# One substitution on 64 partitions for the last two delta rule heads, and the order of adds, casts and splits at the ends of the MLPs and of the last head

## The chip, the cores and the metric

One Trainium2 chip, one core. The metric is device time in microseconds (us). TensorE (PE) multiplies matrices, PEld is its weight load, VectorE (DVE) and ScalarE (ACT) work on tiles, GpSimd (POOL) and SyncE (SP) here mostly issue DMAs. Each engine runs its own instructions in the order in which they were laid down, and waits where an operand or a buffer isn't there yet.

## The reference

Two transformer blocks on 512 tokens of width 1024, in fp32. Cut to what the change touches:

```python
# block 1
h = rmsnorm(x, norm_mix)
gu, gv, q, k, v, gate, b_logit, a_logit = split_cols(h @ w_in, IN_SIZES)
y_a = chunk_spatial_gating(gu, gv, ...)
o = gated_delta_rule(q, k, v, g, beta)     # 4 heads of 128, chunks of 64 tokens
y_b = rmsnorm(o, dn_onorm) * silu(gate)
x = x + concat([y_a, y_b]) @ w_out
m = rmsnorm(mem, norm_mem)                 # 256 memory rows
x = x + cross_attention(rmsnorm(x, norm_xa), m @ w_k, m @ w_v)
x = x + square(relu(rmsnorm(x, norm_ffn) @ w1)) @ w2
# block 2
x = x + mixer2(rmsnorm(x, norm_mix_g))     # mLSTM and sliding window attention
x = x + square(relu(rmsnorm(x, norm_mlp_g) @ w_up)) @ w_down
x = x + sigmoid(rmsnorm(x, norm_ple_g) @ w_ple_gate) * (p @ w_ple_proj)
return rmsnorm(x, final_norm_g)
# in gated_delta_rule, per head and chunk c:
m = strict_lower((k*beta) @ k.T * decay);  a = m + eye(64)
sol = triangular_solve(a, rhs)             # rhs = [v*beta, k*beta*exp(decay)]
```

The kernel takes chunks of 128 tokens, which gives the same o, and inverts their `a`: the 16x16 blocks on the diagonal by forward substitution, then blocks of 32, 64 and 128 by matmuls. A head has four chunks and so 32 blocks of 16x16.

## The kernel before

Every fp32 product is three matmuls on a high and a low half of both operands (`mm3`, L282 to L284). A weight comes by DMA on SP into a raw tile `wr` (L260), ACT casts it to `wh` (L263), DVE subtracts to get `wl` (L264). A granule is 1024x256 of a weight in two such pieces of 128x1024 (512 KB), or one piece for `w_out_b` and `w_out_a`. Outside the MLPs there are two `wr` buffers and three each of `wh` and `wl` (`wtiles`), so a load starts when the `wl` of two pieces before it is done. With each granule the kernel also issues `rate` jobs that build sums of the MLP weights in DRAM by DMA (`job`, `sum_jobs`).

The program is written step by step, and a list scheduler lays the instructions down on each engine, by its own estimates and priorities. `behind(f)` issues what f does after the last matmul so far, `hold(n)` keeps matmuls until n products later, `issue_after(i)` holds an instruction behind another one. With `high_priority(n)` instructions are placed as if they stood n places earlier in the program.

Delta rule (`deltanet`, `dn_head`): a head first makes its scaled q, k, v, the matrix M and QKT (L601 to L646). Then the 16x16 blocks are multiplied out of M on PE (L661), copied by ACT (L671), and spread by four DMAs of 8 KB (L678) so that one block lies on each of 32 partitions. There 15 pairs of DVE operations (L681 multiply, L683 subtract) invert all 32 blocks at once. Four DMAs (L685) bring the result back, L687 places it into `dTb` (T_), and L661, L711, L715 and L720 build up the inverse. Four steps over chunks follow (L735 to L754), the norm and the gate (L758 to L768) and the transposes in `fin` (L773) with the split into `yb` (L327, L328).

Around heads 2 and 3 the matmuls of the memory fill PE: four granules of `xa_wk`, each giving two tiles of 128x256, and four of `xa_wv` (`memory`). The keys are scaled by `bc`, made by `tok_bc`: DVE copies (L354), PE transposes twice (L357), ACT copies (L359), then DVE scales each key tile out of its PSUM bank (L812). Three PSUM banks (`psd`) go round. In the kernel before head 2's substitution and chain stand beside the keys, head 3's beside the values. Then `w_out_b` follows, whose last quarter of the sum (k = 3) needs head 3.

The second GEMM of an MLP (`st_gemm`) makes seven products per granule, added into `x_fm` by DVE (L982) from three PSUM tiles. At the end of an MLP `post` splits each finished tile for the next norm (L327, L328) and sums squares (`sq_acc`, L337 on ACT, L338 on DVE). At the end of MLP 1 this feeds `between`, at the end of MLP 2 `tail`, whose `ple` splits the input p (L324, L325).

Of the kernel before, what the change touches and what calls it, by code (L numbers as in the profile page):

```python
# [12 lines left out]
AF = mybir.ActivationFunctionType  # L13
ALU = mybir.AluOpType
# [18 lines left out]
C_ONORM = C_CONV2 + 32  # L33
# [32 lines left out]
class Kern:  # L66
# [199 lines left out]

    def wgran(self, name, g, n=256, nk=8, pieces=None):

        if self.wx is None:
            self.job()  # L270
        src = self.D[name]
        parts = []
        for h in range(nk // 4):
            parts.append(self.wload(src[g, h], 4, n, pieces if h == 0 else None))
# [45 lines left out]
    def split_sb(self, hi, lo, src, scale=None):  # L320

        nc = self.nc
        if scale is None:
            nc.scalar.copy(hi, src)  # L324
            nc.vector.tensor_tensor(out=lo, in0=src, in1=hi.bitcast(F32), op=ALU.subtract)  # L325
        else:
            nc.scalar.activation(hi, src, AF.Copy, scale=scale)  # L327
            nc.vector.scalar_tensor_tensor(out=lo, in0=src, scalar=scale, in1=hi.bitcast(F32), op0=ALU.mult, op1=ALU.subtract)  # L328

    def sq_acc(self, acc, src, k, scale=None, n=T):  # L330
# [141 lines left out]
    def deltanet(self, xh, xl, rs, bc, mix, mem):  # L472
        nc, mp = self.nc, self.mp
# [16 lines left out]
        qk, v, fins = {}, {}, []  # L490
# [17 lines left out]

        def do_prep(h):
            return self.dn_head(h, *qk[h], v[h], pr, gate, yb_h, yb_l)  # L510

        def do_head(h):
            steps = do_prep(h)
            next(steps)
            fins.append(next(steps))

# [5 lines left out]
        pr = self.dn_prep(ba)  # L522
# [62 lines left out]

    def dn_head(self, h, q, k, v, pr, gate, yb_h, yb_l):

# [84 lines left out]
        Vt, Mo = b4("dV"), b4("dA" + e, 1)  # L672
        bl = lambda t, o: t[0:32].rearrange("p b c -> p (b c)")[:, o:o + 256].rearrange("p (r c) -> p r c", r=16)
        Lb, Tb, Ob = bl(Vt, 0), bl(Vt, 256), bl(Mo, 0)
        V.memset(Tb, 0.0)
        V.memset(flat(Tb)[:, 0::17], 1.0)
        for b in range(NB):
            nc.sync.dma_start(Lb[8 * b:8 * b + 8], Lp[:, b])  # L678
        for j in range(15):
            n, m = 15 - j, j + 1  # L680
            nc.vector.tensor_tensor(out=Ob[:, :n, :m], in0=Lb[:, m:, j:m].broadcast_to([32, n, m]),  # L681
               in1=Tb[:, j:m, :m].broadcast_to([32, n, m]), op=ALU.mult)
            nc.vector.tensor_tensor(out=Tb[:, m:, :m], in0=Tb[:, m:, :m], in1=Ob[:, :n, :m], op=ALU.subtract)  # L683
# [95 lines left out]
    def w_out1(self):  # L779

        xh, xl = self.pair((9, 10)), self.pair((11, 12))
        acc = self.new_acc()

        def ev(o, ps):
            self.add_res(o, ps)
            self.norm_tile(o, xh, xl, acc, "norm_xa")

        for g in range(4):
            self.proj_fm(self.wgran("w_out_b", g, nk=4), *self.yb, (2 * g, 2 * g + 1), ev)
        self.dump("x1", self.x)  # L790
        return xh, xl, acc
# [135 lines left out]
    def st_weights(self, name, g):  # L927
# [36 lines left out]
    def st_gemm(self, name, g, H, o1, post):  # L964
# [60 lines left out]
    def between(self):  # L1025
# [7 lines left out]
        def ev(o):  # L1033
            nonlocal ops
            if o == 0:
                ops = self.pair((2, 3)), self.pair((5, 6)), self.new_acc(), self.t(self.fp, [P, T], "acc2", bufs=1)
            xh, xl, acc, acc2 = ops
            self.split_sb(xh[o], xl[o], self.x[:, o], g12[:, o:o + 1])
            self.sq_acc(acc, self.x[:, o], o)
            self.sq_acc(acc2, self.x[:, o], o, scale=self.vcol("norm_final", o))  # L1040

        def fin():
            self.dump("x3", self.x)
            xh, xl, acc, acc2 = ops
            r1 = self.tok_rs(acc, "rs", power=True)
            ps = self.pss()
            for b in range(NB):
                nc.tensor.matmul(ps[:, b:b + 1], acc2[:, b * P:(b + 1) * P], self.ones[:, 0:1], start=True, stop=True)
            v = self.t(self.tp, [P, NB], "rs2v")
# [331 lines left out]
    def tail(self):  # L1381
# [5 lines left out]
        def ev(o):  # L1387
            nonlocal ops
            if o == 0:
                ops = self.pair((0, 1)), self.pair((4, 7)), self.new_acc()  # L1390
            self.norm_tile(o, *ops, "norm_ple_g_2")

        def ple():
# [207 lines left out]
```

## Time and profile before

| | |
|---|---|
| median of 3 runs | 1700.75 us (1698.43 to 1703.73) |
| profiled execution | 1699.93 us, span 1698.1 us |
| granted TensorE clock | 1.000 over the span |
| PE busy | 1677.7 us, 99% |
| DVE busy | 1207.7 us, 71% |
| ACT busy | 821.5 us, 48% |
| DMA | 205.63 MB, mean 121 GB/s |

A busy share counts overlapping matmuls as one stretch. PE is the engine that is nearly always busy, so the places where it stands still are read one by one: the number in square brackets in a row of the timeline is how long the engine was idle before the instruction, and what ended that.

### The profile page before, as it was taken

How to read it: one execution, taken by the hardware profiler on the slowest of the kernel's cores; microseconds unless marked ns; L12 is line 12 of the kernel's file. 1: busy time of each engine (PE TensorE's matmuls, PEld its weight loads, DVE VectorE, ACT ScalarE, POOL GpSimd, SP SyncE). 2: the span in 40 equal slices, each digit the busy share in tenths (PEclk: the TensorE clock that was granted, in tenths of full speed). 3: DMA queues.
4: the chain of work that ended last, by engine and by line, in shares of the span. 5: the costliest groups of instructions: out<-in, count | busy, mean ns of one | idle time of the engine just before them, and what ended most of it. 6: DMA issues, size and time to landing. Idle time of an engine off the chain costs nothing.

```text
span 1698.1 us, 25916 instructions
## 1 busy us (share of the span) xinstructions
PE 1677.7 (99%) x9916; PEld 1455.5 (86%) x9916; DVE 1207.7 (71%) x2521; ACT 821.5 (48%) x1462; POOL 72.2 (4%) x92
## 2 busy tenths in 40 slices
PE   9999999999999999999999999999999999999998
PEld 8988898887898989889988887788888989898987
DVE  6988886656686868688845569865566767676865
ACT  5355755444444444454444457654234444444554
POOL 0200001000000000000000000000000000000000
PEclk9999999999999999999999999999999999999999
DMA  6321366545546464423333332334464464644331
GB/s 203 101 76 52 96 154 180 135 99 174 121 130 170 127 170 128 132 92 110 103 90 97 100 88 69 94 88 115 118 189 126 130 172 124 172 125 133 100 112 50
DMA packets 81947, 205.63 MB, mean 121 GB/s; under 512 B 13088, under 2 KB 14240, under 8 KB 81824
## 3 DMA queue, kind: packets, MB, share of 16 engines
q1 hardware_dynamic: 62672, 169.29, 31.9%
q0 software_dynamic: 9216, 16.78, 7.1%
q10 hardware_dynamic: 9936, 17.91, 3.8%
q8 instruction: 78, 1.28, 0.3%
q14 instruction: 45, 0.37, 0.1%
HBM read 201.59 MB, written 35.65 MB: 140 GB/s over the span
## 4 chain that ended last, share of the span: by engine, by line
PE 88%; DVE 7%; ACT 2%; issue 1%; DMA 1%; SPq 0%; ACTq 0%; DVEq 0%
PE psd L283 21%; PE psd L284 21%; PE psd L282 21%; PE x L282 5%; PE x L283 5%; PE x L284 5%; DVE wl L264 1%; PE c L661 1%; PE c L607 1%; PE lg L1344 1%; PE po L1371 1%; ACT wh L263 1%; DVE S L437 1%; PE m L1265 1%; DVE acc L338 1%
## 5 line engine op out<-in xcount | busy, mean ns | idle before, releaser
L284 PE MATMUL psd<-S,wl 128*128 128x512 f32 (+1 forms) x1256 | 484.1, 386 | 2.6 <-DVE wl L264 2.5
L282 PE MATMUL psd<-S,wh 128*128 128x512 f32 (+1 forms) x1256 | 483.1, 385 | 0.7 <-ACT S L327 0.7
L283 PE MATMUL psd<-S,wh 128*128 128x512 f32 (+1 forms) x1192 | 458.6, 385 | 1.1 <-DVE S L328 0.8
L284 PEld LDWEIGHTS psd<-S,wl 128*128 128x128 f32 x1256 | 236.3, 188 | 48.1 <-DVE wl L264 3.7
L282 PEld LDWEIGHTS psd<-S,wh 128*128 128x128 f32 x1256 | 236.5, 188 | 45.6 <-ACT S L327 1.1
L264 DVE TENSOR_TENSOR wl<-wr,wh 128x1024 fp32r<-128x1024 f32 (+2 forms) x160 | 192.2, 1201 | 116.3 <-ACT wh L263 115.6
L283 PEld LDWEIGHTS psd<-S,wh 128*128 128x128 f32 x1192 | 224.2, 188 | 44.3 <-DVE S L325 1.5
L263 ACT CAST wh<-wr 128x1024 fp32r<-128x1024 f32 (+2 forms) x160 | 163.9, 1026 | 154.7 <-PE psd L283 107.2
L284 PE MATMUL psd<-wh,S 128*128 128x256 f32 (+2 forms) x480 | 135.8, 283 | 0.0
L282 PE MATMUL psd<-wh,S 128*128 128x256 f32 (+2 forms) x480 | 135.7, 283 | 0.0
L283 PE MATMUL psd<-wl,S 128*128 128x256 f32 (+2 forms) x480 | 135.2, 282 | 0.0
L282 PE MATMUL x<-S,wh 128*128 128x256 f32 x452 | 128.0, 285 | 2.9 <-DVE x_fm L982 2.8
L283 PE MATMUL x<-S,wh 128*128 128x256 f32 x452 | 126.5, 281 | 0.0
L284 PE MATMUL x<-S,wl 128*128 128x256 f32 x452 | 126.0, 280 | 0.0
L283 PE MATMUL psd<-S,whx 128*128 128x512 f32 (+1 forms) x296 | 107.8, 364 | 1.0 <-DVE S L325 0.9
L282 PE MATMUL psd<-S,whx 128*128 128x512 f32 (+1 forms) x296 | 107.8, 365 | 0.0
L284 PE MATMUL psd<-S,wlx 128*128 128x512 f32 (+1 forms) x296 | 107.5, 363 | 0.0
L982 DVE TENSOR_TENSOR x_fm<-x_fm,x 128x256 f32<-128x256 f32 x192 | 78.5, 415 | 27.4 <-PE x L284 27.1
L282 PEld LDWEIGHTS psd<-wh,S 128*128 128x128 f32 x480 | 90.4, 189 | 0.3
L283 PEld LDWEIGHTS psd<-wl,S 128*128 128x128 f32 x480 | 90.3, 188 | 0.3
L284 PEld LDWEIGHTS psd<-wh,S 128*128 128x128 f32 x480 | 90.4, 188 | 0.1
L282 PEld LDWEIGHTS x<-S,wh 128*128 128x128 f32 x452 | 84.8, 188 | 5.8 <-DVE x_fm L982 3.1
(455 smaller groups left out, 3176.3 us busy)
## 6 DMA issues: line engine op xcount, KB each, us to landing
wrx<-in_ffn_w_dram SPq DMA_DIRECT2D x32, 512.0 KB
wrx<-in_w_up_dram SPq DMA_DIRECT2D x20, 512.0 KB
wr<-in_w_in_qk_dram SPq DMA_DIRECT2D x16, 512.0 KB
sums_ffn_w<-in_ffn_w_dram ACTq DMA_DIRECT2D x32, 256.0 KB
wr<-in_ffn_w_dram SPq DMA_DIRECT2D x16, 512.0 KB
sums_w_down<-in_w_down_dram ACTq DMA_DIRECT2D x32, 256.0 KB
wr<-in_w_in_v_dram SPq DMA_DIRECT2D x12, 512.0 KB
wr<-in_w_up_dram SPq DMA_DIRECT2D x12, 512.0 KB
```

Source lines behind the costliest of these rows:

```text
L263: self.last_cast = nc.scalar.copy(hi[:, c], raw[:, c])
L264: nc.vector.tensor_tensor(out=lo[:, c], in0=raw[:, c], in1=hi[:, c].bitcast(F32), op=ALU.subtract)
L282: mm(ps, ah, bh, start=first, stop=False, skip_group_check=more)
L283: mm(ps, ah, bl, start=False, stop=False, skip_group_check=more)
L284: self.last_mm = mm(ps, al, bh, start=False, stop=last, skip_group_check=more)
L338: nc.vector.tensor_tensor(out=acc, in0=acc, in1=sq, op=ALU.add)
L437: nc.vector.tensor_scalar(out=d, in0=d, scalar1=ag[:, j, 0:1], scalar2=r[:, j:j + 1], op0=ALU.subtract, op1=ALU.mult)
L607: nc.tensor.matmul(blk(ps, b), lhs(b), rhs(b), start=True, stop=True)
L661: nc.tensor.matmul(ps[:, b * n:(b + 1) * n], lhs[:, b], rhs(b), start=True, stop=True)
L982: TT(out=x[n][t], in0=x[n][t], in1=ps, op=op)
L1265: nc.tensor.matmul(pX[:, :W], PT[:, tt], va[:, tt], start=True, stop=True)
L1344: nc.tensor.matmul(ps[:, i, K0:], qs[:, 2 * e2 + i, cs], kd[:, w, kc], start=(w == 0), stop=(w == 1))
```

## The change

Heads 2 and 3 put their blocks into one tile: head 2's on partitions 0 to 31, head 3's on 32 to 63. The 15 pairs run once, on 64 partitions, after both heads' blocks have arrived. Head 2's chain now runs beside head 3's. `do_head` is still used for heads 0 and 1. The first granule of `w_out_b` does k = 0, 1, 2 for both of its tiles and then k = 3 for both, and the cast of its second granule is held behind the cast of `yb`. In the MLPs the adds into `x_fm` and the weight splits get priority 400, the norm splits at the end 200, and p's splits and the copies of the p product 400. The matmuls of the statistics in `between` are held for 8 products, `tok_bc` for 21 instead of 16. Line numbers of the changed kernel differ from those before: L264 is L265 there, L338 L340, L354 L356, L357 L359, L661 L670, L681 and L683 are L696 and L698, L685 and L687 are L701 and L704, L812 is L840, L982 is L1013.

```diff
-    def wload(self, src, kt, n, pieces=None):
+    def wload(self, src, kt, n, pieces=None, behind=None):
...
-            self.last_cast = nc.scalar.copy(hi[:, c], raw[:, c])
+            with self.tc.issue_after(behind.ins) if behind else nullcontext():
+                self.last_cast = nc.scalar.copy(hi[:, c], raw[:, c])
...
-    def norm_tile(self, k, xh, xl, acc, gname):
-
-        self.split_sb(xh[k], xl[k], self.x[:, k], self.vcol(gname, k))
+    def norm_tile(self, k, xh, xl, acc, gname, ahead=0):
+
+        with self.tc.high_priority(ahead):
+            self.split_sb(xh[k], xl[k], self.x[:, k], self.vcol(gname, k))
...
-        do_head(2)
+
+        two = do_prep(2, 64)
+        next(two)
         do_wa(1)
-        prep = do_prep(3)
-        next(prep)
+        both = next(two)
+        three = do_prep(3, 64, both)
+        for steps in (three, three, two, three):
+            next(steps)
         do_wa(2)
         do_wa(3)
...
-        fins.append(next(prep))
-        for _ in range(5):
+        for steps in (two, three):
+            fins.append(next(steps))
+            next(mem)
+        for _ in range(3):
             next(mem)
...
+        tiles = first or (Vt, Mo)
+        Lb, Tb, Ob = bl(tiles[0], 0), bl(tiles[0], 256), bl(tiles[1], 0)
+        at = 32 if first else 0
...
         for b in range(NB):
-            nc.sync.dma_start(Lb[8 * b:8 * b + 8], Lp[:, b])
...
+            nc.sync.dma_start(Lb[at + 8 * b:at + 8 * b + 8], Lp[:, b])
+        if rows == 64 and not first:
+            yield tiles
+        else:
+            for j in range(15):
+                n, m = 15 - j, j + 1
+                nc.vector.tensor_tensor(out=Ob[:, :n, :m], in0=Lb[:, m:, j:m].broadcast_to([rows, n, m]),
+                   in1=Tb[:, j:m, :m].broadcast_to([rows, n, m]), op=ALU.mult)
+                nc.vector.tensor_tensor(out=Tb[:, m:, :m], in0=Tb[:, m:, :m], in1=Ob[:, :n, :m], op=ALU.subtract)
+            yield
         for b in range(NB):
-            nc.sync.dma_start(Rp[:, b], Tb[8 * b:8 * b + 8])
+            nc.sync.dma_start(Rp[:, b], Tb[at + 8 * b:at + 8 * b + 8])
+        yield
...
+        wh, wl = self.wgran("w_out_b", 0, nk=4)
+        (yh, yl), ps = self.yb, [self.psd() for _ in range(2)]
+        for ks in ((0, 1, 2), (3,)):
+            for j in range(2):
+                for k in ks:
+                    c = slice(j * P, (j + 1) * P)
+                    self.mm3(ps[j], wh[k][:, c], wl[k][:, c], yh[k], yl[k], k == 0, k == 3)
...
+            w = self.wgran("w_out_b", g, nk=4, behind=self.yb_cast if g == 1 else None)
...
         def split(raw, hi, lo, c=slice(0, 2)):
-            self.split_sb(hi[:, c], lo[:, c], raw[:, c])
+            with self.tc.high_priority(400):
+                self.split_sb(hi[:, c], lo[:, c], raw[:, c])
...
         def add(n, t, ps, op=ALU.add):
-            TT(out=x[n][t], in0=x[n][t], in1=ps, op=op)
+            with self.tc.high_priority(400):
+                TT(out=x[n][t], in0=x[n][t], in1=ps, op=op)
...
-            with self.hold(16):
+            with self.hold(21):
```

On DVE, where the second piece of the first key granule is turned into `wl` (`wl_2756` before, `wl_2630` after), before:

```order
L681 TENSOR_TENSOR dA_402_2284<-dV_2283 32x3x13
L643 TENSOR_TENSOR dM_2576<-c_462_2571,slg_2546 128x512
L683 TENSOR_TENSOR dV_2283<-dV_2283,dA_402_2284 32x3x13
L646 TENSOR_TENSOR QKT_2583<-c_464_2578,slg_2546 128x512
L681 TENSOR_TENSOR dA_402_2284<-dV_2283 32x2x14
L189 TENSOR_TENSOR rsmt_2726<-rsmy_2725 128x2
L264 TENSOR_TENSOR wl_2756<-wr_2754,wh_2755 128x1024
```

After:

```order
L386 SCALAR_TENSOR_TENSOR dq_2093<-sq_2139,e_371_2134 128x512
L473 TENSOR_TENSOR x_fm<-psd_2488,x_fm 128x512
L771 TENSOR_TENSOR do_1817<-do_1817,c_317_1855 128x128
L265 TENSOR_TENSOR wl_2630<-wr_2628,wh_2629 128x1024
L778 TENSOR_TENSOR dso_1860<-dso_1860,dsc_1866 128x4
L783 TENSOR_TENSOR do_1817<-do_1817,gate_713 128x512
```

The piece stood behind 13 pairs of head 2's substitution and M and QKT of head 3; now it stands ahead of both, among the end of head 1.

On PE, where the key scale is transposed (`pss`); `psd_3036` before and `psd_2858` after is the first tile of the second key granule. Before:

```order
L284 MATMUL psd_3036<-S_477_2662,wl_3026 128x256
L282 MATMUL psd_3036<-S_477_2662,wh_3025 128x256
L357 MATMUL pss_2740<-masks,e_500_2738 128x128 x2
L283 MATMUL psd_3036<-S_478_2663,wh_3025 128x256
L284 MATMUL psd_3036<-S_477_2662,wl_3026 128x256
```

After:

```order
L284 MATMUL psd_2858<-S_444_2537,wh_2853 128x256
L285 MATMUL psd_2858<-S_443_2536,wl_2854 128x256
L359 MATMUL pss_2614<-masks,e_466_2612 128x128 x2
L283 MATMUL psd_2887<-S_443_2536,wh_2847 128x256
L284 MATMUL psd_2887<-S_444_2537,wh_2847 128x256
```

The transposes moved from the middle of the third key tile to its end; the next matmul writes a fourth tile, into the bank that the first one holds until it is scaled.

On DVE, the same place and the start of the scaled tiles, after (before, the copy `e` had only the `wl` of the piece that PE was using ahead of it):

```order
L189 TENSOR_TENSOR rsmt_2600<-rsmy_2599 128x2
L265 TENSOR_TENSOR wl_3066<-wr_3064,wh_3065 128x1024
L190 SCALAR_TENSOR_TENSOR rsmt_2600<-rsmt_2600,rsmv_2596 128x2
L329 SCALAR_TENSOR_TENSOR S_177_1232<-c_481_2692,vec,S_176_1231 128x512
L191 SCALAR_TENSOR_TENSOR rsmy_2599<-rsmt_2600,rsmy_2599 128x2
L356 COPY e_466_2612<-rsmy_2599 128x256
L840 TENSOR_TENSOR e_478_2659<-psd_2634,bc_2617 128x256
L696 TENSOR_TENSOR dA_407_2318<-dV_2317 64x15
```

The copy stands behind `wl_3066`, the first piece of the third key granule, and the shared substitution begins behind the first scaled tile. It ends on DVE here (`wl_3217` is the second piece of the first value granule):

```order
L265 TENSOR_TENSOR wl_3211<-wr_3209,wh_3210 128x1024
L698 TENSOR_TENSOR dV_2317<-dV_2317,dA_407_2318 64x5x11
L326 TENSOR_TENSOR S_470_2620<-e_581_3130,S_469_2619 128x256
...
L696 TENSOR_TENSOR dA_407_2318<-dV_2317 64x15
L698 TENSOR_TENSOR dV_2317<-dV_2317,dA_407_2318 64x15
L674 TENSOR_TENSOR dA_407_2318<-dM_2255,masks 128x512
L265 TENSOR_TENSOR wl_3217<-wr_3215,wh_3216 128x1024
```

On DVE at the end of MLP 1 (`x_7767` before is `x_7735` after), before:

```order
L328 SCALAR_TENSOR_TENSOR S_1202_7591<-x_fm,g_804_4657,S_1200_7589 128x512
L325 TENSOR_TENSOR wl_7764<-wr_7742,wh_7763 128x1024
L338 TENSOR_TENSOR acc_7593<-acc_7593,sq_7736 128x512
L338 TENSOR_TENSOR acc_1205_7594<-acc_1205_7594,sq_7739 128x512
L982 TENSOR_TENSOR x_fm<-x_fm,x_7767 128x256
L982 TENSOR_TENSOR x_fm<-x_fm,x_7768 128x256
```

After:

```order
L329 SCALAR_TENSOR_TENSOR S_1202_7559<-x_fm,g_804_4625,S_1200_7557 128x512
L1013 TENSOR_TENSOR x_fm<-x_fm,x_7600 128x256
L326 TENSOR_TENSOR wlx_7848<-wrx_7846,whx_7847 128x1024
L326 TENSOR_TENSOR wl_7732<-wr_7710,wh_7731 128x1024
L1013 TENSOR_TENSOR x_fm<-x_fm,x_7735 128x256
```

The sums of squares of that tile moved to some 25 places later, and the add stands behind weight splits alone.

## Rows read from the trace of the kernel before

**Rows 1.** The page's list of engines: busy time, share of the span, instructions.

```profile
PE 1677.7 (99%) x9916; PEld 1455.5 (86%) x9916; DVE 1207.7 (71%) x2521; ACT 821.5 (48%) x1462; POOL 72.2 (4%) x92
```

**Rows 2.** The waits of PE over the whole span: engine, what it was to do, what ended the wait; us in total, times, longest.

```profile
PE x L282 <- DVE x_fm L982: 2.8, 3, 1.7
PE psd L284 <- DVE wl L264: 2.5, 3, 1.2
```

**Rows 3.** A table by stretch: the stretch and its length, busy time of PE, PEld, DVE, ACT and POOL (instructions), granted clock, DMA share, GB/s. The stretches are the key granules, the value granules, the first of `w_out_b` and the end of MLP 1.

```profile
212.47:252.02 39.55, 37.50 (x316) 35.92 (x314) 33.84 (x125) 19.71 (x49) 3.24 (x4) 1.00 0.62 155
252.02:287.94 35.92, 35.57 (x297) 33.80 (x296) 22.91 (x64) 19.88 (x45) 3.23 (x4) 1.00 0.65 169
287.94:320.00 32.06, 30.53 (x132) 24.23 (x131) 23.77 (x32) 17.27 (x25) 4.06 (x5) 1.00 0.78 191
740.00:775.00 35.00, 33.06 (x272) 32.28 (x271) 32.40 (x55) 20.29 (x29) 0.00 (x0) 1.00 0.31 98
```

**Rows 4.** The timeline of all engines in the first key granule.

```profile
217.40 0.36 PE L283 MATMUL psd<-S,wh 128*128 128x256 f32 x1
217.66 1.21 DVE L264 TENSOR_TENSOR wl<-wr,wh 128x1024 fp32r<-128x1024 f32 x1
218.93 0.33 SPq L260 DMA_DIRECT2D wr<-in_xa_wk_dram  x1
218.93 0.39 PE L284 MATMUL psd<-S,wl 128*128 128x256 f32 x1 [1.16 <-DVE wl L264]
```

**Rows 5.** The timeline of ACT over the same granule and the next: the casts of the two pieces concerned, and the copy of the key scale.

```profile
203.79 1.06 ACT L263 CAST wh<-wr 128x1024 fp32r<-128x1024 f32 x1 [0.34 <-PE psd L283]
222.93 1.05 ACT L263 CAST wh<-wr 128x1024 fp32r<-128x1024 f32 x1
224.25 0.38 ACT L359 COPY bc<-pss 128x256 f32<-128x256 f32 x1 [0.27 <-PE pss L357]
```

**Rows 6.** The timeline of all engines in the second key granule, around the transposes of the key scale.

```profile
223.43 0.29 DVE L354 COPY e<-rsmy 128x256 f32<-128x256 f32 x1
223.77 0.44 PE L357 MATMUL pss<-masks,e 128*128 128x128 f32 x2
224.28 0.28 PE L282 MATMUL psd<-S,wh 128*128 128x256 f32 x1
224.29 1.22 DVE L264 TENSOR_TENSOR wl<-wr,wh 128x1024 fp32r<-128x1024 f32 x1
224.40 0.28 PE L283 MATMUL psd<-S,wh 128*128 128x256 f32 x1
225.56 0.39 PE L284 MATMUL psd<-S,wl 128*128 128x256 f32 x1 [0.89 <-DVE wl L264]
225.63 0.42 DVE L812 TENSOR_TENSOR e<-psd,bc 128x256 f32<-128x256 f32 x1
```

**Rows 7.** The substitutions of heads 2 and 3, from the view of line L681: count, shortest, median and longest duration in ns, first and last start.

```profile
L681 DVE TENSOR_TENSOR dA<-dV x30: 155/192/214, 204.6 to 249.6; 32x15 f32<-32x15 f32 x4, 32x28 f32<-32x28 f32 x4, 32x39 f32<-32x39 f32 x4, 32x48 f32<-32x48 f32 x4
```

**Rows 8.** The timeline of DVE: head 3's last subtract, and the placing of its T_.

```profile
249.76 0.16 DVE L683 TENSOR_TENSOR dV<-dV,dA 32x15 f32<-32x15 f32 x1
254.96 0.28 DVE L687 TENSOR_TENSOR dTb<-dY,masks 128x128 f32<-128x128 f32 x1
```

**Rows 9.** The timeline of SP's queue: start, time to the end of the last of the group, count. L260 loads pieces of weights, L685 brings T_ back.

```profile
241.27 6.56 SPq L260 DMA_DIRECT2D wr<-in_xa_wv_dram  x3
249.99 2.68 SPq L685 DMA_DIRECT2D dY<-dV  x4
...
282.54 0.33 SPq L260 DMA_DIRECT2D wr<-in_w_out_b_dram  x1
```

**Rows 10.** The timeline of ACT: casts that waited for their load, and the cast of head 3's `yb` (L327).

```profile
245.17 1.05 ACT L263 CAST wh<-wr 128x1024 fp32r<-128x1024 f32 x1 [0.78 <-DMA wr<-in_xa_wv_dram]
252.66 1.05 ACT L263 CAST wh<-wr 128x1024 fp32r<-128x1024 f32 x1 [0.77 <-DMA wr<-in_xa_wv_dram]
289.20 1.05 ACT L263 CAST wh<-wr 128x1024 fp32r<-128x1024 f32 x1 [2.07 <-DMA wr<-in_w_out_b_dram]
290.15 0.68 ACT L327 ACTIVATE S<-c,vec 128x512 fp32r<-128x512 f32 x1
```

**Rows 11.** The timeline of PE and DVE in the first granule of `w_out_b`.

```profile
290.28 1.23 DVE L264 TENSOR_TENSOR wl<-wr,wh 128x1024 fp32r<-128x1024 f32 x1 [4.53 <-ACT wh L263]
290.88 0.50 PE L282 MATMUL psd<-S,wh 128*128 128x512 f32 x1 [0.70 <-ACT S L327]
291.42 0.74 DVE L328 SCALAR_TENSOR_TENSOR S<-c,vec,S 128x512 fp32r<-128x512 f32 x1
292.22 0.50 PE L283 MATMUL psd<-S,wh 128*128 128x512 f32 x1 [0.83 <-DVE S L328]
```

**Rows 12.** The timeline of PE and DVE at the end of MLP 1.

```profile
757.24 1.28 DVE L338 TENSOR_TENSOR acc<-acc,sq 128x512 f32<-128x512 f32 x2
758.45 0.74 DVE L982 TENSOR_TENSOR x_fm<-x_fm,x 128x256 f32<-128x256 f32 x2
758.91 0.38 PE L282 MATMUL x<-S,wh 128*128 128x256 f32 x1 [1.69 <-DVE x_fm L982]
```

**Rows 13.** The timeline of PE at the end of MLP 2 and in the first product of `ple`.

```profile
1623.41 0.36 PE L282 MATMUL x<-S,wh 128*128 128x256 f32 x1 [0.86 <-DVE x_fm L982]
...
1631.83 0.50 PE L283 MATMUL psd<-S,whx 128*128 128x512 f32 x1 [0.95 <-DVE S L325]
```

More of the change, by code (lines that the diff above doesn't have):

```diff
@@ L273, in wgran @@
         for h in range(nk // 4):
-            parts.append(self.wload(src[g, h], 4, n, pieces if h == 0 else None))
+            parts.append(self.wload(src[g, h], 4, n, pieces if h == 0 else None, behind))
         hi = [parts[k // 4][0][:, k % 4] for k in range(nk)]
@@ L323, in split_sb @@
         if scale is None:
-            nc.scalar.copy(hi, src)
+            cast = nc.scalar.copy(hi, src)
             nc.vector.tensor_tensor(out=lo, in0=src, in1=hi.bitcast(F32), op=ALU.subtract)
         else:
-            nc.scalar.activation(hi, src, AF.Copy, scale=scale)
+            cast = nc.scalar.activation(hi, src, AF.Copy, scale=scale)
             nc.vector.scalar_tensor_tensor(out=lo, in0=src, scalar=scale, in1=hi.bitcast(F32), op0=ALU.mult, op1=ALU.subtract)
+        return cast
     def sq_acc(self, acc, src, k, scale=None, n=T):
@@ L507, in do_wa, with do_prep @@
             self.proj_fm(self.wgran("w_out_a", g, nk=4), *self.ya, (2 * g, 2 * g + 1), self.add_res)
-        def do_prep(h):
-            return self.dn_head(h, *qk[h], v[h], pr, gate, yb_h, yb_l)
+        def do_prep(h, rows, first=None):
+            return self.dn_head(h, *qk[h], v[h], pr, gate, yb_h, yb_l, rows, first)
         def do_head(h):
-            steps = do_prep(h)
-            next(steps)
-            fins.append(next(steps))
+            *_, fin = do_prep(h, 32)
+            fins.append(fin)
         gate = self.t(mp, [P, NB, T], "gate", bufs=1)
@@ L584, in dn_prep, with dn_head @@
         return dict(beta=beta, g=g, edec=ee[:, 0], edl=ee[:, 1], wl=ee[:, 2])
-    def dn_head(self, h, q, k, v, pr, gate, yb_h, yb_l):
+    def dn_head(self, h, q, k, v, pr, gate, yb_h, yb_l, rows, first=None):
         nc, mp = self.nc, self.mp
@@ L672, in dn_head @@
         Vt, Mo = b4("dV"), b4("dA" + e, 1)
[L673 to L676, printed above, removed]
-        for b in range(NB):
-            nc.sync.dma_start(Lb[8 * b:8 * b + 8], Lp[:, b])
[L679 to L683, printed above, removed]
+        bl = lambda t, o: t[0:rows].rearrange("p b c -> p (b c)")[:, o:o + 256].rearrange("p (r c) -> p r c", r=16)
+        tiles = first or (Vt, Mo)
+        Lb, Tb, Ob = bl(tiles[0], 0), bl(tiles[0], 256), bl(tiles[1], 0)
+        at = 32 if first else 0
+        if not first:
+            V.memset(Tb, 0.0)
+            V.memset(flat(Tb)[:, 0::17], 1.0)
+        for b in range(NB):
+            nc.sync.dma_start(Lb[at + 8 * b:at + 8 * b + 8], Lp[:, b])
[8 more added lines that the diff above has]
+            yield
         for b in range(NB):
-            nc.sync.dma_start(Rp[:, b], Tb[8 * b:8 * b + 8])
+            nc.sync.dma_start(Rp[:, b], Tb[at + 8 * b:at + 8 * b + 8])
+        yield
         T_ = b32("dTb")
@@ L958, in st_weights @@
         C = load(s[:, 0:1], a[:, 3:4])
-        nc.vector.tensor_tensor(out=A[0], in0=A[0], in1=B[0], op=ALU.add)
+        with self.tc.high_priority(400):
+            nc.vector.tensor_tensor(out=A[0], in0=A[0], in1=B[0], op=ALU.add)
         s1, a22 = split(*C)
@@ L1037, in ev @@
             xh, xl, acc, acc2 = ops
-            self.split_sb(xh[o], xl[o], self.x[:, o], g12[:, o:o + 1])
+            with self.tc.high_priority(200):
+                self.split_sb(xh[o], xl[o], self.x[:, o], g12[:, o:o + 1])
             self.sq_acc(acc, self.x[:, o], o)
@@ L1044, in fin @@
             xh, xl, acc, acc2 = ops
[L1045 to L1048, printed above, removed]
+            with self.hold(8):
+                r1 = self.tok_rs(acc, "rs", power=True)
+                ps = self.pss()
+                for b in range(NB):
+                    nc.tensor.matmul(ps[:, b:b + 1], acc2[:, b * P:(b + 1) * P], self.ones[:, 0:1], start=True, stop=True)
             v = self.t(self.tp, [P, NB], "rs2v")
@@ L1397, in ple @@
             for i in range(2):
-                self.split_sb(ph[:, i], ph[:, 2 + i], raw[:, i])
+                with self.tc.high_priority(400):
+                    self.split_sb(ph[:, i], ph[:, 2 + i], raw[:, i])
             pp = [self.slot(i, [P, 4, T]) for i in (2, 3)]
             def ev_p(o, ps):
-                nc.scalar.copy(pp[o // 4][:, o % 4], ps)
+                with self.tc.high_priority(400):
+                    nc.scalar.copy(pp[o // 4][:, o % 4], ps)
             for g in range(4):
```

13 lines of the change are left out of this document (8 added, 5 removed).

## The prediction

> **What bounds the kernel.** I first read the list of engines: PE is busy for 99% of the span, the next engine, DVE, for 71% [rows 1]. So the time is PE's work plus PE's standstills, and a change that removes no matmuls can win only standstills. The clock is at its upper level (1.00, which is 2.4 GHz) in every stretch that I use [rows 3], so no part of this is a clock effect. Then I read PE's waits by what ended them [rows 2]: two kinds stand out, the add into `x_fm` (2.8 us in three waits) and `wl` (2.5 us in three). The timeline puts each at its place: two in the key granules of the memory [rows 4, 6], two in the first granule of `w_out_b` [rows 11], one at the end of MLP 1 [rows 12], two at the end of MLP 2 [rows 13]. These seven are all the change can aim at. Their idle times are 1.16, 0.89, 0.70, 0.83, 1.69, 0.86 and 0.95, in sum 7.08 us.
>
> An idle time understates the loss a little. In the first key granule one matmul starts at 217.40 and the next at 218.93 [rows 4]; such matmuls otherwise follow each other every 0.12 us, as from 224.28 to 224.40 [rows 6], so the loss is 1.41 against an idle time of 1.16. In the second it is 225.56 - 224.40 - 0.12 = 1.04 against 0.89 [rows 6]. The factor is 1.2 for both together, and I use it throughout: 7.08 x 1.2 = 8.5 us is the most that can be won. That is 0.5% of the time.
>
> **The MLP ends.** Before, two sums of squares (L338, 1.28 us at 757.24) stand ahead of the add that PE waits for (758.45), and PE starts 0.46 us after that add starts [rows 12]. The order of the changed kernel has the add behind weight splits alone. Two pairs of sums go from ahead of it (1.28 us each), and one weight split more comes (some 1.2 us, as the `wl` in [rows 4]), so it starts some 1.3 us earlier, and the wait of 1.69 is gone but for some 0.3. DVE is busy for 32.4 of the 35 us there [rows 3], so it is DVE that ends last, and the moved sums must fit before the statistics need them; behind the last product PE has the next mixer's matmuls, and `hold` puts the statistics 8 products later, which is cover enough. I take 1.69 x 1.2 = 2.0, the 0.3 within the rounding of the factor. MLP 2 has the same wait (0.86) and p's split (0.95) [rows 13]; both splits and adds are moved ahead of sums of squares: 1.81 x 1.2 = 2.2. Bounds for the two ends together: 4.2 if nothing else is late, 1.0 if the weight split ahead of the add is as late as the sums were.
>
> **`w_out_b`.** The cast of the second granule's weight waited 2.07 us for its load and ran from 289.20 to 290.25, ahead of the cast of `yb` at 290.15 [rows 10]; its `wl` (290.28, 1.23 us) ran ahead of the low half of `yb` at 291.42 [rows 11]. The new order holds that cast behind `yb`'s and gives PE 18 matmuls of k = 0 to 2 before it needs `yb`. Both waits go: 1.53 x 1.2 = 1.8. The price is that the second granule's weight is ready later: cast 1.05 and `wl` 1.23 start after `yb` instead of before, while PE has only the six k = 3 matmuls as cover, 1.4 us at twice the 0.12 us of tiles half as wide. I put a leftover of 0.3 against it, with bounds 0 and 0.9.
>
> **The heads: what goes.** The first key wait comes because `wl` of a piece cast at 203.79 [rows 5] ran only at 217.66 [rows 4], behind head 2's substitution and head 3's preparation. The second follows from it: the load into that raw buffer could be issued only when this `wl` was done, at 218.93 [rows 4], its cast came at 222.93 [rows 5], its `wl` at 224.29 [rows 6]. In the new order both pieces stand earlier, so 2.05 x 1.2 = 2.5 us goes.
>
> Thirty DVE operations go too, at a median of 192 ns [rows 7]: up to 30 x 0.19 = 5.8 us of DVE. No row shows such an operation on 64 partitions. The bounds are 0.15 us (the shortest on 32) and 0.42 us (a 128x256 operation, L812 [rows 6], which moves more elements per partition); I take it as unchanged, since the element counts per partition are those of before. It is not PE's time: DVE is busy for 33.8 of 39.6 us among the keys and 22.9 of 35.9 among the values [rows 3], and pays only where PE waits for it.
>
> **The heads: what comes.** Head 2's chain leaves the keys. From the second key granule to the first value granule PE now has nothing but granules: 48 matmuls of 0.12 us, 5.8 us each. Three new waits follow.
>
> First, the key scale. Before, 14 matmuls and a short product stood between the transposes (223.77) and the next tile, and the copy by ACT (224.25, 0.38) and the first scaled tile (225.63, 0.42) hid behind them [rows 5, 6]. Now the transposes stand at the end of the third tile, and the fourth goes into the first one's bank. From the transposes' start to the end of the copy is 224.63 - 223.77 = 0.86, and 0.42 for scaling, so 1.3 us is the least; about 0.1 of it is the transposes' own issue. If the copy `e` (0.29) also waits behind `wl_3066`, whose load cannot be issued before `wl_2848` is done, it is 2.9. I take 1.9.
>
> Second, the supply of weights. A raw buffer is taken from the issue of its load to the end of its `wl`. Loads took 245.17 - 241.27 = 3.9 us, 252.66 - 247.50 = 5.16 us (the third of that group is issued 0.33 before its end) and 289.20 - 282.54 = 6.66 us [rows 9, 10]. With 1.05 for the cast and 1.22 for `wl`, a pair of buffers gives one granule in 6.2, 7.4 or 8.9 us, against 5.8 us of PE. Three `wh` and `wl` tiles are ahead at the start, so the first deficit is absorbed. Over four granules the deficit is 4 x 0.4 = 1.6, 4 x 1.6 = 6.4 or 4 x 3.1 = 12.4, less some 4 us of stock (the first wait above gives the loads 1.9, the three tiles ahead the rest): 0, 2.4 or 8.4. I take 2.0, near the two loads among these granules.
>
> Third, T_. Head 3's last subtract ended at 249.92 and T_ was placed at 254.96, 5.0 us later, through four DMA issues of 0.65 [rows 8, 9]. Now eight issues stand together, and the loads of the second value granule's last piece are behind them. Head 2's four go first, so its T_ is no later than 5.0 us after the substitution, but the substitution itself now ends between `wl_3211` and `wl_3217`, when PE is at the first value granule. PE's cover is that granule, 5.8 us. I take 1.0 for T_ and 1.0 for `wl_3217` and for the two chains side by side among the values, with bounds 0 and 5 together.
>
> What is added is then 1.9 + 2.0 + 2.0 = 5.9 us, against 2.5 that goes.
>
> The Trainium skill has a rule that would make the second wait nothing: in "DMA: Bandwidth & Descriptors", section "Anatomy of one DMA — SWDGE (gpsimd) path", a DMA costs about 2 us plus its bytes at 436 GB/s, which by that page is an estimate of 3.2 us for 512 KB. The rows of loads above say 3.9 to 6.7 us, for loads issued by SP and beside other traffic, and so decide for more than the page gives; by the page a granule would take 5.5 us, there would be no deficit, and the sum below would come to 1695.6.
>
> **The sum.** The profiled execution took 1699.93 us, 0.8 under the median. 1699.93 - 4.2 (MLP ends) - 1.8 + 0.3 (`w_out_b`) - 2.5 + 5.9 (heads) = 1697.6. I say 1697.5.
>
> **Rivals.**
> *All waits go and no new one counts.* For it: DVE has 5.8 us less to do where it is busiest, the three tiles of stock, loads of 3.9 us, and two chains beside each other hide each other's latency. Against: the bank that the fourth key tile needs. 1699.93 - 8.5 + 0.3 + 1.3 = 1693.0; with the key scale hidden too, 1691.
>
> *The memory weights run dry.* The same DMA work of the keys (0.62 of the engines over 39.6 us [rows 3]) now falls into some 28 us, which would be a share of 0.62 x 39.55 / 28 = 0.88. At a share of 0.78 a load took 6.7 us [rows 3, 9, 10]. Then the supply term is 8.4 instead of 2.0, and since the substitution's pairs stand between the `wl` on DVE, it ends later by as much, and T_ and both chains with it: 3 to 5 us more among the values, as little stands there to fill in. 1697.6 + 6.4 + 4 = 1708. It decides from loads of about 6 us on; against it are the loads of 3.9 and 5.2 among these granules.
>
> *The order changes and the ends stay.* If the adds at the MLP ends wait just as long for the weight splits now ahead of them, 3.2 of the 4.2 stays: 1697.6 + 3.2 = 1700.8. For it speaks DVE's 32.4 of 35 us [rows 3].
>
> **The chances.** This kernel's runs differ by about 0.3% (5.3 us between the lowest and highest of three), so 0.3%, 5.1 us, is what a measurement can tell from no change: faster means under 1695.65, slower over 1705.85. My forecast, 1694 to 1701, has 0.50, of which some 0.07 lies under 1695.65; all waits gone 0.28; weights run dry 0.13; the ends stay 0.09. Faster 0.35, same 0.52, slower 0.13. The range leaves out the far ends of the second and third case: 1691 to 1704.
>
> **What would show it.** At the MLP ends, an add into `x_fm` with no idle time of PE behind it; in `w_out_b` no wait for the split of `yb`; in the first key granule no wait for `wl`. Against the gain: a wait of PE of 1 to 3 us behind the key transposes (on the scaled tile), waits for `wl` in the third key granule to the second value granule, and one at the first L670 of the values. Were there none of these three, the first rival holds; were the loads among the keys at 6 us or more, the second. I would be wrong in kind if the time moved outside these places.

## The result and the profile after

The changed kernel takes 1705.3 us (median of 20 runs, 1698.59 to 1713.07), the kernel before 1699.52 (20 runs, 1698.26 to 1703.73): ratio 1.0034, 95% interval [1.0024, 1.0044]. Slower by 0.34%, where I had forecast 1697.5 and said 1691 to 1704. Its runs lie 14.5 us apart, before's 5.5, and they follow the mean granted clock: from 1698.59 us at 0.998 to 1713.07 at 0.992, correlation -0.91, some 1.5 us more for each 0.001 less. The line through the 20 runs gives 1697.5 us at a clock of 1.000.

The profiled execution took 1709.43 us, span 1707.6. The table by stretch answers to [rows 3] (the columns are the same; the clock is the third number from the end):

```profile
212.00:242.80 30.80, 29.16 (x241) 28.38 (x240) 25.36 (x83) 14.41 (x31) 2.42 (x3) 1.00 0.62 161
242.80:245.40 2.60, 0.70 (x5) 0.30 (x3) 2.46 (x7) 0.82 (x1) 0.00 (x0) 0.95 0.91 304
245.40:248.70 3.30, 3.30 (x16) 3.30 (x16) 1.40 (x3) 1.82 (x3) 0.81 (x1) 0.52 0.17 33
248.70:255.30 6.60, 6.08 (x52) 5.70 (x51) 3.52 (x11) 0.86 (x3) 0.00 (x0) 1.00 0.74 199
255.30:275.60 20.30, 20.30 (x101) 19.22 (x101) 6.49 (x12) 5.88 (x13) 0.81 (x1) 0.50 0.29 80
275.60:320.00 44.40, 43.98 (x291) 38.53 (x291) 30.27 (x78) 26.90 (x63) 4.86 (x6) 1.00 0.58 148
740.00:785.00 45.00, 45.00 (x356) 43.64 (x356) 40.31 (x68) 27.20 (x38) 0.00 (x0) 1.00 0.25 83
```

PE stands still for most of 242.8 to 245.4, then runs for 3.3 us and, 6.6 us later, for 20.3 us at the lower of its two levels (0.50, 1.2 GHz). It is busy all that time, so the idle columns show nothing: 101 instructions in 20.3 us, against 297 in 35.9 before [rows 3]. The 128x256 matmuls follow each other every 0.21 us there (12 of them from 245.94 to 248.50), instead of every 0.12. As PE is busy throughout, I estimate that the share of the clock that was missing is lost time: 20.3 x 0.50 + 3.3 x 0.48 = 11.7 us. 1709.43 - 11.7 = 1697.7, where the sum of my steps was 1697.6.

The timeline of PE shows the waits that stand there now, against [rows 4, 6]:

```profile
226.36 0.39 PE L283 MATMUL psd<-S,wh 128*128 128x256 f32 x1 [0.92 <-DVE e L840]
237.35 0.38 PE L285 MATMUL psd<-S,wl 128*128 128x256 f32 x1 [0.49 <-DVE wl L265]
243.67 0.39 PE L283 MATMUL psd<-wh,S 128*128 128x256 f32 x1 [0.61 <-ACT wh L264]
245.34 0.58 PE L284 MATMUL psd<-wl,S 128*128 128x256 f32 x1 [1.28 <-DVE wl L265]
249.34 1.08 PE L670 MATMUL c<-dTb,dT 128*128 128x32 f32 x8 [0.41 <-DVE dTb L704]
```

In order: the key scale's bank (226.36), the second piece of the fourth key granule's weight (237.35; some expectations below call it the third), the second piece of the first value granule's (243.67 for `wh`, 245.34 for `wl`), and T_ (249.34). These are the three kinds that I had named. SP, ACT and DVE show why the two pieces are late:

```profile
230.34 0.33 SPq L260 DMA_DIRECT2D wr<-in_xa_wk_dram  x1
234.65 1.05 ACT L264 CAST wh<-wr 128x1024 fp32r<-128x1024 f32 x1
236.09 1.21 DVE L265 TENSOR_TENSOR wl<-wr,wh 128x1024 fp32r<-128x1024 f32 x1
237.32 0.33 SPq L260 DMA_DIRECT2D wr<-in_xa_wv_dram  x1
242.57 1.05 ACT L264 CAST wh<-wr 128x1024 fp32r<-128x1024 f32 x1 [0.33 <-DMA wr<-in_xa_wv_dram]
244.07 1.22 DVE L265 TENSOR_TENSOR wl<-wr,wh 128x1024 fp32r<-128x1024 f32 x1
```

The two pieces share a raw buffer. The second load is issued when the first piece's `wl` is done (237.30), and the cast waits for it until 242.57, 5.2 us later. Another 0.45 us between that cast's end (243.62) and its `wl` is DVE's order.

Of the waits of [rows 11 to 13] none of more than 0.4 us is left.

### The profile page after: what moved, and what is told of

It reads as the page before. It is cut to its first block, busy times and chain, and to the rows that moved or that the text cites. A ratio compares the mean times of both kernels' runs of the same rounds, so it can differ in the third digit from the quotient of the medians.

```text
span 1707.6 us, 25851 instructions
## 1 busy us (share of the span) xinstructions
PE 1689.8 (99%) x9916; PEld 1466.6 (86%) x9916; DVE 1209.2 (71%) x2489; ACT 821.4 (48%) x1462; POOL 71.9 (4%) x92
## 3 DMA queue, kind: packets, MB, share of 16 engines
q8 instruction: 78, 1.28, 0.3%
## 4 chain that ended last, share of the span: by engine, by line
PE 88%; DVE 6%; ACT 3%; DMA 2%; issue 1%; SPq 0%; ACTq 0%; DVEq 0%
PE psd L285 20%; PE psd L284 20%; PE psd L283 20%; PE x L283 6%; PE x L284 5%; PE x L285 5%; DVE wl L265 1%; PE c L670 1%; PE c L616 1%; ACT wh L264 1%; PE lg L1377 1%; PE po L1404 1%; DMA wr<-in_xa_wv_dram 1%; DVE S L440 1%; PE m L1298 1%
## 5 line engine op out<-in xcount | busy, mean ns | idle before, releaser
L265 DVE TENSOR_TENSOR wl<-wr,wh 128x1024 fp32r<-128x1024 f32 (+2 forms) x160 | 192.1, 1201 | 116.6 <-ACT wh L264 116.1
L264 ACT CAST wh<-wr 128x1024 fp32r<-128x1024 f32 (+2 forms) x160 | 163.9, 1026 | 157.4 <-PE psd L284 107.8
L284 PE MATMUL psd<-wl,S 128*128 128x256 f32 (+2 forms) x480 | 138.8, 289 | 1.3 <-DVE wl L265 1.3
L283 PE MATMUL psd<-wh,S 128*128 128x256 f32 (+2 forms) x480 | 138.1, 288 | 0.6 <-ACT wh L264 0.6
L285 PE MATMUL psd<-wh,S 128*128 128x256 f32 (+2 forms) x480 | 138.2, 288 | 0.0
L1013 DVE TENSOR_TENSOR x_fm<-x_fm,x 128x256 f32<-128x256 f32 x192 | 79.5, 417 | 24.8 <-PE x L285 23.3
L283 PEld LDWEIGHTS psd<-wh,S 128*128 128x128 f32 x480 | 92.7, 193 | 1.4 <-ACT wh L264 0.8
L285 PEld LDWEIGHTS psd<-wh,S 128*128 128x128 f32 x480 | 92.9, 194 | 0.0
L283 PE MATMUL x<-S,whx 128*128 128x256 f32 x316 | 90.5, 287 | 0.0
```

Of the source, the lines that this page charges most:

```text
L283: mm(ps, ah, bh, start=first, stop=False, skip_group_check=more)
L284: mm(ps, ah, bl, start=False, stop=False, skip_group_check=more)
L285: self.last_mm = mm(ps, al, bh, start=False, stop=last, skip_group_check=more)
```

## The experiments

Each is compared with runs of the kernel before on the same chip.

**The two halves of the change.** First everything but the shared substitution (`deltanet` and `dn_head` as before), then the shared substitution alone.

> Everything of the change but the shared substitution: heads 2 and 3 as before. Theory (the lost time is TensorE's clock at its lower level after PE stood still in the first value granule, and the rest of my sum holds): clock 1.000 in every run, the four waits at the MLP ends and the two in w_out_b gone, the two waits for wl among the keys kept: 1699.5 - 5.7 = 1693.8 us, 1692.5 to 1695. Rival (the new order at the MLP ends or in w_out_b costs time somewhere else): 1699 us or more.

Measured: 1695.16 us (7 runs), ratio 0.9969 [0.9958, 0.9981], clock 0.998 to 1.000.

> The shared substitution alone, with the old order of adds, casts and splits. Theory: the clock falls in the heads as in the whole change, mean 0.991 to 0.999 and different from run to run; 1699.5 + 3 of new waits net and 3 to 12 for the clock: 1703 to 1715 us, median 1709. Rival (the clock's fall needs the order parts too): clock 1.000, about 1702.5 us with a narrow spread.

Measured: 1713.11 us (4 runs), ratio 1.0073 [1.0057, 1.0088], clock 0.991 to 0.995. The order parts win 5.0 us, a little less than the 5.7 expected; the shared substitution alone loses 13, and its clock is down in all four runs. The two don't simply add up: the whole change lost 5.8. In the profile of the shared substitution alone:

```profile
212.00:254.40 42.40, 36.68 (x299) 35.16 (x297) 32.17 (x98) 16.98 (x33) 3.23 (x4) 1.00 0.63 164
254.40:267.20 12.80, 12.80 (x62) 12.54 (x61) 5.09 (x10) 4.02 (x9) 0.81 (x1) 0.50 0.46 104
```

**Cures for the supply of weights**, each on the whole change. No DMA jobs among keys and values:

```diff
-        self.rate = 2
+        self.rate = 0
```

> The whole change, but no DMA jobs for the MLP sums are issued while the memory's keys and values are made (rate 0 there; they are issued later). It leaves out no computation. Theory (the pause of PE in the first value granule is the weights' supply, lengthened by the other DMA traffic): loads fall from 5 to 6 us to some 4, the waits for wl and wh in the third key and first value granule, 3 us together, shrink below 1.5, the clock stays above 0.998 in most runs, 1696 to 1700 us. Rival (the loads take as long by themselves, or the wait is DVE behind the substitution): the same waits, the clock as in the whole change, 1701 to 1712 us.

Measured: 1700.07 us, ratio 1.0002 [0.9991, 1.0012], clock 0.994 to 1.000. The waits for weights shrank from 3.0 to 1.6 us (start to start); the loads that ACT waited for took 3.7 to 5.1 us, against 5.2 to 7.2 in the changed kernel. The clock was still at 0.996 or below in six of ten runs. In the profile it fell at 251.9 for 10.2 us, 8.6 us after the last of those waits, with PE busy in between, on value tiles and the two chains. Then a third raw buffer (every third piece goes there), alone and with no jobs:

```diff
+        raw = self.slot(7, [P, kt, n]) if third else fs[0]()
```

> The whole change with a third raw weight buffer for the memory's keys and values (a free tile). Theory (PE's pause in the first value granule is the weights' supply through two raw buffers, and lets the clock fall): the waits for wh and wl from the third key to the first value granule shrink from 3 us to below 1, the wait for T_ may grow by up to 1.5; where the sum of the pauses stays under 2 us, clock 0.998 or above in most runs, 1694 to 1700 us. Rival (DVE's queue behind the substitution makes wl late, not the load): the pause stays at 1.5 to 2.3 us and the clock falls as in the whole change, 1701 to 1711 us.

Measured: 1700.82 us, ratio 1.0022 [0.9998, 1.0047]; seven runs at 0.996 to 0.998 and 1699 to 1702 us, three at 0.989 to 0.990 and 1713 to 1715. No wait for weights was left, and both my cases were wrong: PE waited 3.3 us for T_ instead. On SP and then DVE:

```profile
238.21 0.33 SPq L262 DMA_DIRECT2D S<-in_xa_wv_dram  x1
240.79 6.76 SPq L704 DMA_DIRECT2D dY<-dV  x8
...
247.71 0.29 DVE L707 TENSOR_TENSOR dTb<-dY,masks 128x128 f32<-128x128 f32 x1 [1.21 <-DMA dY<-dV]
```

From the end of the last subtract (240.55, 0.17) to T_ it is then 7.0 us, instead of 5.6 in the changed kernel (243.43 to 249.00) and 5.0 for one head before [rows 8]. A load is issued 2.6 us ahead of the small DMAs of T_, but so it is in the changed kernel (240.93 and 243.50), so that load alone doesn't explain it. The next run shows what the jobs have to do with it.

> The whole change with the third raw buffer and without the DMA jobs among keys and values, both cures of the supply at once. Theory: no wait for weights from the third key granule on, only the key scale (1.5 us) and T_ (up to 1.5 us) left; clock 0.998 to 1.000, 1693 to 1698 us. Rival (the packed two chains with their short matmuls let the clock fall by themselves): mean clock 0.992 to 0.997, 1699 to 1708 us though no wait for weights is left.

Measured: 1697.38 us, ratio 0.9980 [0.9971, 0.9990], clock 0.997 to 1.000. Both cures together: PE waits 0.6 us (start to start) for T_ and for no weights, and T_ takes 4.2 us, though the load is again issued 2.6 us ahead of its DMAs (236.62 and 239.20). The edits of this run and the one before differ in the jobs alone. In the profile the clock falls no more among keys and values, though the two chains with their short matmuls are as before; it fell for 3.4 us at 291.7, behind a wait in `w_out_b` (0.78 us). The other nine runs have a clock of 0.997 to 1.000 and no profile. So the rival, that the chains let the clock fall by themselves, is not borne out: its 1699 to 1708 us did not come.

The third buffer with the order parts alone:

> The order parts alone with the third raw buffer. Theory (the two key waits come of the order on DVE): they stay, clock 0.999 to 1.000, 1694 to 1696 us as with the order parts alone. Rival (the second of them is the raw buffer, since its load was issued only when the piece before was done): one of them goes, 1693.5 to 1694.5 us.

Measured: 1702.9 us, ratio 1.0016 [1.0004, 1.0027]. Neither: the two key waits stay, 1.4 and 1.0 us start to start, and PE and DVE wait 3.3 us each for T_ of head 3, again with loads and jobs under way; why it is that much later than with two buffers isn't shown. Clock 0.994 to 0.999. The second key wait stays although the load of its piece is now issued at 206.22 instead of 218.97 (the order parts alone) and its cast runs at 216.01: its `wl` still runs only at 224.54. So that wait is DVE's order, not the raw buffer, as the prediction had it.

**More PE work for each weight.** Two granules of `w_out_a` moved from before the memory to between the keys:

```diff
             next(mem)
+            do_wa(len(fins) - 1)
```

> The whole change with two granules of w_out_a (5.6 us of PE from one piece of weights each) moved from before the memory to between its key granules. Theory (with head 2's chain gone the keys run faster than their weights arrive): the waits for wh and wl in the third key to first value granules shrink below 1 us in sum, the clock stays at 0.998 or above in most runs, 1693 to 1698 us. Rival (PE waits for the DVE queue behind the substitution, or for T_): the waits stay 3 us or more and the clock falls, 1700 to 1712 us.

Measured: 1705 to 1711 us in three runs, ratio 1.0058 [1.0038, 1.0078], clock 0.993 to 0.996. The expected gain did not come. A fourth run, the profiled one, took 2735.72 us at a mean clock of 0.555, so where PE waits here stays open.

**The old key waits alone.** Priority 150 for the first two key granules, on the order parts:

> The order parts, heads as before, and the weights of the first two key granules with priority 150, so that their wl stands ahead of most of head 2's substitution on DVE. Theory (the two waits for wl among the keys are a matter of the order on DVE alone): both go, 2.4 us, clock 1.000: 1695.2 - 2.4 = 1692.8 us, 1691.5 to 1694.5. Rival (the substitution is then late and T_ waits instead): 1694.5 to 1698 us.

Measured: 1703.41 us, ratio 1.0024 [1.0013, 1.0035], clock 0.993 to 0.997. The rival, and worse. PE came earlier to head 2's T_, which came 0.9 us later (226.40, against 225.47 with the order parts alone), and the clock fell at 226.8 for 17 us:

```profile
226.75 1.86 PE L664 MATMUL c<-dTb,dT 128*128 128x32 f32 x8 [1.81 <-DVE dTb L690]
228.97 1.92 PE L664 MATMUL c<-dY,dV 128*128 128x32 f32 x8 [0.36 <-ACT dY L701]
231.26 1.06 PE L664 MATMUL c<-dTb,dA 128*128 128x32 f32 x4 [0.38 <-DVE dTb L704]
```

So taking these two waits away alone wins nothing here: another wait takes their place, and the some 8 us that this run loses against the order parts are about what the clock cost (an estimate: 17 x 0.50 = 8.5).

**PE's standing still and the clock.** Twelve matmuls to nowhere in the changed kernel's longest pause:

```diff
+                            self.nc.tensor.matmul(pf[:, :n], xh[0][:, c], wh[0][:, :n], start=True, stop=True)
```

> The whole change with 12 matmuls of 128x256 into a PSUM tile that nobody reads, put in front of the second half of the first value tile, where PE stood for 2.3 us; they add 1.4 us of PE work that the wait covers. Theory (it is PE's standing still that lets the clock fall): the clock stays at 1.000 or falls for a shorter time, 1697 to 1701 us. Rival (the clock falls by the DMA or DVE load there, or by the many short matmuls of the two chains): mean clock 0.991 to 0.997 as in the whole change and 1702 to 1712 us.

Measured: 1701.95 us, ratio 1.0012 [1.0003, 1.0022], clock 0.997 to 0.998. The fall in the profile is shorter (3.4 us), but 1.28 us of the wait for `wl` stayed and T_ was waited for (2.61 us), so PE stood still for longer in sum, and it is no clean test. A pause put into the order parts is one:

```diff
+            for _ in range(slow):
+                nc.vector.tensor_scalar(out=raw[:, c], in0=raw[:, c], scalar1=1.0, scalar2=None, op0=ALU.mult)
```

> The order parts alone (heads as before, clock 1.000 in its runs), with five needless DVE passes over the raw second piece of the first value granule ahead of its cast, so that PE stands still there for some 2 to 4 us once. Theory (a pause of PE in this stretch is enough to let the clock fall): the clock falls to its lower level within some 10 us after the pause, mean 0.992 to 0.998, and the time is that of the order parts, 1695.2, plus the pause plus 3 to 10 for the clock: 1700 to 1710 us. Rival (the clock falls by what is special to the shared substitution, its run of key granules without other work or its two chains at once): clock 1.000 and 1697 to 1699.5 us.

Measured: 1699.23 us, ratio 0.9999 [0.9989, 1.0009], clock 0.995 to 0.998 in all ten runs. The pause was smaller than meant, and on T_ (0.98 us where the order parts alone wait 0.3), but behind it the clock fell:

```profile
254.00:257.40 3.40, 2.55 (x19) 2.35 (x20) 3.09 (x10) 2.24 (x3) 0.00 (x0) 0.95 0.05 8
257.40:263.60 6.20, 6.20 (x31) 6.20 (x31) 3.05 (x9) 2.02 (x7) 0.81 (x1) 0.50 0.91 222
263.60:300.00 36.40, 36.09 (x264) 32.94 (x264) 21.67 (x48) 21.18 (x44) 4.05 (x5) 1.00 0.72 179
```

> The same with three passes, a pause of some 0 to 1.5 us. Theory: a smaller pause, like the 1.1 and 1.4 us that the kernel before has without a fall, lets the clock fall in no run or in few: 0.999 to 1.000, 1695 to 1697.5 us. Rival (any pause here does it): as with five passes.

Measured: 1694.9 us, ratio 0.9973 [0.9964, 0.9982]; no pause was added. Nine of ten runs at 0.999 or 1.000. The tenth, 1699.47 us at 0.995, is the profiled one: its clock fell at 226.4 for 13.7 us, right behind the two key waits that before has too. So the clock falls behind these waits now and then; of the 13 runs of the kernel before that were taken with the next experiment, one took 1705.81 us at 0.995.

The same passes over a piece in the first GEMM of MLP 1, far from the heads:

> The order parts alone, with fourteen needless DVE passes of 0.67 us over one raw piece of a granule in the first GEMM of MLP 1, so that PE stands still there once, for some 2 to 6 us, among long matmuls and far from the heads. Theory in its strong form (any pause of this size lets the clock fall): the clock falls soon after it in most runs, mean below 0.998, and the time is 1695.2 plus the pause plus 2 to 10 us. Rival (the pause counts only beside the short matmuls of the heads, as the 1.7 us at the end of MLP 1 in the kernel before went without a fall): clock 0.999 to 1.000, and 1695.2 plus the pause alone, 1697 to 1701 us.

Measured: 1694.78 us, ratio 0.9970 [0.9959, 0.9980], clock 0.998 to 1.000: fourteen passes of 0.69 us on DVE were not felt by PE.

> As with fourteen passes, which PE did not feel, now twenty: four us more of DVE ahead of that piece, so a pause of PE of some 1 to 3 us in MLP 1. Theory in its strong form (a pause of this size lets the clock fall anywhere): mean clock 0.998 or lower in most runs, 1698 to 1705 us. Rival (it counts only beside the heads' short matmuls): clock 0.999 to 1.000, 1695 plus the pause, 1696 to 1698 us.

Twenty passes. Measured: 1695.02 us (6 runs), ratio 0.9970 [0.9957, 0.9982]; not felt either.

> The same with thirty passes, a pause of some 6 to 10 us. Strong form: the clock falls in all runs, mean 0.993 to 0.998, 1695 plus the pause plus 3 to 10 us: 1704 to 1715. Rival (no pause among long matmuls lets it fall): clock 0.999 to 1.000, 1701 to 1705 us.

Measured: 1702.08 us, ratio 1.0009 [1.0000, 1.0019], clock 0.996 to 0.998. PE stood for 4.1 us, and the clock was down when it went on:

```profile
622.75:626.30 3.55, 0.40 (x2) 0.00 (x0) 3.24 (x5) 0.14 (x1) 0.00 (x0) 1.00 0.00 0
626.30:633.20 6.90, 5.90 (x13) 4.22 (x14) 3.50 (x4) 2.80 (x3) 0.81 (x1) 0.51 0.63 154
```

> Twenty-seven passes: by the 4.1 us at thirty and 0.69 us a pass, a pause of PE of some 2 us among long matmuls, as long as the longest in the changed kernel. If such a pause is enough by itself: clock 0.998 or lower in most runs, 1695 + 2 + 2 to 4: 1699 to 1701 us. If it counts only beside the heads' short matmuls and their further waits: clock 0.999 to 1.000, 1696.5 to 1698 us.

Measured: 1697.66 us, ratio 0.9988 [0.9972, 1.0004]. A pause of 1.9 us: nine runs of ten at 0.998 or 0.999, its profile without a fall, one run at 0.993 and 1708.98.

> Twenty-eight passes, a pause of some 2.7 us. If enough by itself: clock 0.998 or lower in most runs, 1699.5 to 1702 us. If not: clock 0.999 to 1.000, 1697 to 1698.5 us.

Measured: 1698.99 us, ratio 0.9998 [0.9986, 1.0010]. A pause of 2.7 us: eight runs at 0.998 or 0.999, two at 0.994 and 0.996; in the profile the clock was down for 3.4 us, from 626.2.

A pause alone can be enough, then: at 4.1 us the mean clock was down in all ten runs, and at 2.7 us the profiled run shows a fall. 1.9 us among long matmuls mostly passed without a fall, while with 1.0 us beside the heads' short matmuls, some 30 us after the two key waits, the mean clock was 0.995 to 0.998 in all ten runs. Which of the two neighbours counts there, the short matmuls or the earlier waits, and why the clock stays down 3 us in one run and 20 in another, is not settled. Nor does the fall always follow at once: in the changed kernel (second fall) and in the run without jobs PE was busy for 6.0 and 8.6 us after its last wait when the clock fell.

## Why the prediction was wrong

The step that failed is in the first part: "so no part of this is a clock effect". The clock was at its upper level throughout the profile of the kernel before, and I took that as given for a kernel whose pauses stand closer together. The waits that I then priced, of PE for weights and T_ among keys and values, came about. But behind them the clock fell for 3.3 and 20.3 us, which by the estimate above cost 11.7 us in the profiled run, a term that neither the sum nor any of my rivals has. It comes with the shared substitution (alone, its clock was 0.991 to 0.995 in all four runs; with the order parts alone it was below 0.998 in none of seven), and with the waits for weights cured the same change took 1697.38 us.

By step:
- *MLP ends and `w_out_b`*: right in place and nearly in size. 5.7 us forecast (4.2 + 1.8 - 0.3), 5.0 measured with the order parts alone, and again 5.1 and 4.9 in the runs with passes that PE did not feel.
- *Key scale*: 1.9 us taken; now 0.23 + 0.92 us of idle time around the transposes, 1.5 start to start.
- *Supply of weights*: 2.0 taken; 0.49 + 0.61 + 1.28 = 2.4 us of idle time, 3.0 start to start, mis-sized by 1.0. The cures by jobs and by a third buffer show that it is mostly the loads. The 1.28 us are the wait for `wl_3217`, for which the next term held a part too; in sum the two terms took 4.0 and measured 3.6.
- *T_ and the chains*: 2.0 taken; 0.41 us idle, 0.6 start to start, mis-sized by 1.4 the other way. T_ came 5.6 us after the substitution, where I had said 5.0 at most. A wait that I hadn't named, 0.49 us, stands at 209.8 in the preparation of a head.
- *The key waits that go*: 2.5 taken, and they are gone from the trace; but taken away alone they gave nothing, as T_ was next in line. That the second follows from the raw buffer is wrong: with its load 12.8 us earlier it stayed.
- *The operations saved on DVE*: the shared substitution's last operations take 0.17 us on 64 partitions (64x15), against 0.16 on 32 [rows 8], and the largest 0.22 (64x64), against 0.21 before [rows 7]; no wait of PE shows a gain from them, as forecast.
- *Weights run dry*: the rival nearest in time (1708) by another mechanism: its term for the supply was 8.4 us, measured 3.0; the rest of the loss is the clock. Of the loads that ACT waited for, one took 7.2 us (among the keys) and three 5.2 to 5.5.
- *The Trainium skill's rule for a load* (page "DMA: Bandwidth & Descriptors", section "Anatomy of one DMA — SWDGE (gpsimd) path"), by which 512 KB is an estimate of 3.2 us: the trace after doesn't agree, with 5.2 to 7.2 us for the loads, issued by SP, that ACT waited for.

That the sum without the clock comes to 1697.5 is partly luck, since the terms were off by up to 1.4 us in opposite directions. By the line through the 20 runs it is some 1699 us at the mean clock of the kernel before (0.999), within 0.6 us of that kernel.

The version that beats both is the order parts alone: 1695.16 us, 0.31% below the kernel before and 0.6% below the whole change.

## What to carry to other kernels

Sum up not only each standstill of TensorE that a change makes, but also ask where they stand: here waits of 2.8 us in sum within 13 us (the changed kernel) were followed by more than 23 us at the lower clock, and one of 1.0 us in the heads by more than 6 us, which cost more than the waits themselves. A time that scatters from run to run with the mean granted clock is the sign, and the clock's column by stretch shows the place while the idle times show nothing. And before taking a wait away, look at what would be waited for next: here the key waits hid a DVE and DMA chain.

## What was new about the hardware

- The clock was given back after anything from some 3 us (a 2.7 us pause in MLP 1) to some 20 us (the changed kernel), with PE busy all that time in both, and one kernel gave mean clocks from 0.991 to 0.999 over 20 runs.
- Eight DMAs of 8 KB, four for each head, needed 7.0 us from the last subtract to the first use of the first four's result with the jobs' traffic, and 4.2 us without it. In both runs a load of 512 KB was issued 2.6 us ahead of them. Without the jobs:

```profile
238.97 0.17 DVE L701 TENSOR_TENSOR dV<-dV,dA 64x15 f32<-64x15 f32 x1
243.32 0.29 DVE L707 TENSOR_TENSOR dTb<-dY,masks 128x128 f32<-128x128 f32 x1 [0.52 <-DMA dY<-dV]
```
